# Layer 0's second MLP chunk in seven products for both column halves, with more weight sums in DRAM and wider squares in attention

## The chip, the cores and the metric

One core of one Trainium2 chip runs the whole program. The metric is the device time in microseconds (us) of one execution; a profile of one execution says where it goes. The engines are TensorE (PE, with its weight loads as PEld), VectorE (DVE), ScalarE (ACT), GpSimd (POOL) and SyncE (SP, which here only issues transfers).

## The reference

A trunk of two layers works on x of 256 positions by 2048 channels in float32. Layer 0 mixes by multi-scale pooling and grouped-query attention, layer 1 by a chunkwise mLSTM; behind each mixer stands a gated MLP. Cut to what the change touches:

```python
proj = h @ w_in_ab[e]                          # layer 0: pooling | queries | keys | values
q = apply_rope(rms_norm(q, q_norm[e]), cos, sin)
k = apply_rope(rms_norm(k, k_norm[e]), cos, sin)
...
def conv_ffn(x, w_up, conv_w, conv_b, w_down): # both layers, D_FF = 5632
    u = x @ w_up
    ...                                        # width-3 depthwise convolution over positions
    gate, val = jnp.split(u, 2, axis=-1)
    return (jax.nn.silu(gate) * val) @ w_down
```

## The kernel before, in words

**Precision.** Every float32 product is three matmuls in a reduced format: each operand is split into a high and a low part, and high x high, high x low and low x high are added up in PSUM (the low x low term is left out). Weights come in chunks of 128 x 1024 (512 KB). `Stream` loads them on SP's queue (L114, tile `w`, six chunks ahead), ScalarE casts the high part (L134) and VectorE subtracts for the low part (L135, tile `hl`, two chunks ahead of TensorE, four buffers). All matmuls of products stand on L272.

**The MLP.** The 5632 inner channels are 44 tiles of 128, in K chunks of 4, 8, 8, 8, 8 and 8 tiles (`FCH`). An `up` step makes one tile of gate and value (64 matmuls, four weight chunks) and, on ScalarE and VectorE, the convolution and the gating (L438 to L1019). While the tiles of chunk c + 1 are made, chunk c goes through the down projection. `_ffn_plan` writes the order: up tiles, and in the slots between them the units of the down projection.

**Seven products.** Where a chunk and a column half h (1024 of the 2048 columns) are in `BOTH`, the down projection treats a pair of K tiles, the two blocks of 128 positions and two column blocks of 512 as a 2 x 2 times 2 x 2 product, with seven block products in place of eight. `unit` runs them: an A unit four products for each pair, a B unit three. `combine` makes the combinations of the left operand (L1025 to L1032), `drain` adds the sums in PSUM to accumulators or to x (L1086, L1088), and `total` adds it all up at the end. Where a half is not in `BOTH`, `down` runs the eight products directly (tile `dn`, 48 matmuls for one chunk and one column block) and `residual` (L448) adds them to x. The halves of a chunk that are both in seven products run in units of two pairs; with one half alone they run in units of one pair.

**Sums of weights.** An A unit also needs sums of weight blocks. They come in two ways. On the fly (`Sum` and `Chain`): SP loads one part (L119), an accumulating transfer on POOL's queue adds the other (L120), and VectorE makes the other two sums of a pair in the chunk itself (L130, L131). Or from DRAM: `premix` builds all four sums ahead of time in a scratch tile `m`, in steps that each wait for a matmul (L484): two copies issued by ScalarE, three accumulating steps issued by POOL, each in two halves of the partitions. SP then loads `m` like any weight chunk. A premix starts every 26 units of the planner's clock (about a microsecond each) for the first eight, then every 45, and takes five such gaps of 26. `_ffn_weights` says which pairs are premixed.

**Attention.** `block` takes the projected keys or queries of four heads (tile `kproj` or `qproj`, two position blocks of 512 columns in PSUM), squares them with a sum for each head (eight ScalarE instructions of 128 columns, L519), and applies gains and rotation on VectorE (L528, L529, L531). TensorE transposes the result (L563). It runs for the keys and for three groups of queries.

TensorE runs in the order in which the program is written; the order on the other engines is set by a scheduler.

Of the kernel before, what the change touches and what calls it, by code (L numbers as in the profile page):

```python
# [9 lines left out]
F32 = mybir.dt.float32  # L10
F32R = mybir.dt.float32r
AF = mybir.ActivationFunctionType
ALU = mybir.AluOpType
AX = mybir.AxisListType
PSUM = bass.MemoryType.PSUM

P = 128
# [14 lines left out]
FT = DFF // P  # L32
FCH = [4, 8, 8, 8, 8, 8]
CH = 8
BOTH = ((0, 2, 3, 4), (0, 1, 2, 3, 4))
LAST = (4, 4)

PASSES = (
    ("A1 B1 A0 B0", "A1 B1", "A1 B1 A0 B0", "A1 B1 A0 B0", "A0 A1 A1+ B0 B1 B1+"),
    ("A1 B1 A0 B0", "A1 B1 A0 B0", "A1 B1 A0 B0", "A1 B1 A0 B0", "A0 A1 A1+ B0 B1 B1+"),  # L40
)
NEG = -1.0e30
# [50 lines left out]
class Stream:  # L93
# [60 lines left out]
    def next(self):  # L154
        i = self.at
        self.ahead(i)
        self.at += 1
        return self.hl.pop(i)
# [58 lines left out]
def trunk(ctx: ExitStack, tc: tile.TileContext, gx, xT, xn, call, catt, cml, weights, mixes, out):  # L217
    nc = tc.nc
    v, a, g, pe = nc.vector, nc.scalar, nc.gpsimd, nc.tensor

    def pool(name, bufs, **kw):
        return ctx.enter_context(tc.tile_pool(name=name, bufs=bufs, **kw))
# [9 lines left out]
    sm1 = pool("small1", 1)  # L232
# [41 lines left out]
    def rsqrt(ss, n, scale, name):  # L274

        t = smp.tile([P, n], F32, tag=f"rv{n}", name=f"rv_{name}")
        v.tensor_scalar(t, ss, scale, EPS, ALU.mult, ALU.add)
        y = smp.tile([P, n], F32, tag=f"ry{n}", name=f"ry_{name}")
        g.tensor_tensor(y, t, mhalf[:, :n], ALU.pow)
        e = smp.tile([P, n], F32, tag=f"re{n}", name=f"re_{name}")  # L280
        v.tensor_mul(e, y, y)
        v.tensor_mul(e, e, t)
        v.tensor_scalar(e, e, -0.5, 1.5, ALU.mult, ALU.add)
        v.tensor_mul(e, e, y)
        return e
# [156 lines left out]
    def bc(ap, n):  # L442
        return ap.unsqueeze(1).to_broadcast([ap.shape[0], n, ap.shape[1]])
# [27 lines left out]
    def paced(ins):  # L471

        tc.add_manual_dep(ins.ins, last_mm[0].ins.name, now, reason="paced")

    def premix(layer, gap, late, n):

        def one(i, s0, s1, r, made):
            m = scratch.tile([P, 2, CH * P], F32, tag=f"m{layer}{i}", name=f"m{layer}_{i}")
            h = CH * P // 2
            steps = [(nc.scalar, m[:, 0], s0, {}), (nc.scalar, m[:, 1], r, {}), (g, m[:, 0], s1, add),  # L480
                     (g, m[:, 1, :h], m[:, 0, :h], add), (g, m[:, 1, h:], m[:, 1, :h], add)]
            for n, (eng, to, src, kw) in enumerate(steps):
                for p in range(0, P, P // 2):
                    paced(eng.dma_start(to[p : p + P // 2], src[p : p + P // 2], **kw))  # L484
                    yield (0.1, 0.6, 0.6, 0.6, 0.6)[n] * gap
            for j in range(2):
                made[j].ap = m[:, j]

        for i, e in enumerate(mixes[layer]):
            wv.aside(one(i, *e), min(i + 1, n) * gap + max(i + 1 - n, 0) * late)  # L490
# [8 lines left out]
    def attention_layer(norm, nxt):  # L499
        with ExitStack() as es:  # L500
# [11 lines left out]
            def block(ps, ti, dst, name):  # L512

                rot = tp.tile([P, 2, 512], F32, tag="rot", name=f"rot_{name}")
                ss = smp.tile([P, 8], F32, tag="qss", name=f"qss_{name}")
                sq = sm1.tile([P, 512], F32, tag="sq", name=f"hsq_{name}")[:, :P]
                for t in range(2):
                    for h in range(4):
                        a.activation(sq, ps[:, t, h * P : h * P + P], AF.Square,  # L519
                                     accum_out=ss[:, 4 * t + h : 4 * t + h + 1])  # L520
                for t in range(2):
                    t2 = t1p.tile([P, 512], F32, tag=f"qt2{t}", name=f"qt2_{name}{t}")
                    q4 = ps[:, t, :].rearrange("p (h a b c) -> p h a b c", h=4, a=2, b=2)
                    o4 = t2.rearrange("p (h a b c) -> p h a b c", h=4, a=2, b=2)
                    gs = tab[:, ti + 1, t].rearrange("p (a b c) -> p a b c", a=2, b=2)
                    for b in range(2):
                        gb = gs[:, :, b, :].unsqueeze(1).to_broadcast([P, 4, 2, 32])
                        v.tensor_mul(o4[:, :, :, b, :], q4[:, :, :, 1 - b, :], gb)  # L528
                    v.tensor_mul(rot[:, t, :].rearrange("p (h d) -> p h d", h=4),  # L529
                                 ps[:, t, :].rearrange("p (h d) -> p h d", h=4), bc(tab[:, ti, t], 4))  # L530
                    v.tensor_add(rot[:, t, :], rot[:, t, :], t2)  # L531
                yield 9.5

                def scales():

                    s3 = ss.rearrange("p (t h) -> p t h", t=2)
                    rc = norm.rcol.unsqueeze(2).to_broadcast([P, 2, 4])
                    for _ in range(2):
                        v.tensor_mul(s3, s3, rc)
                    rq = rsqrt(ss, 8, 1.0 / HD, f"q{name}")  # L540
                    r3 = rq.rearrange("p (t h) -> p t h", t=2)
                    v.tensor_mul(r3, r3, rc)
                    return rq

                rq = None
                if name == "k":
                    yield from wv.wait(lambda: norm.blocks == NB)
                    fin = norm.finish()
                    yield next(fin)
                    rq = scales()  # L550
                    yield 4.0
                    for t in range(2):
                        r4 = rot[:, t, :].rearrange("p (h d) -> p h d", h=4)
                        v.tensor_mul(r4, r4, rq[:, 4 * t : 4 * t + 4].unsqueeze(2).to_broadcast([P, 4, P]))
                    yield 3.0
                for h2 in range(2):
                    if name != "k":
                        yield from wv.take("qt")
                    tr = psp.tile([P, 2, S], F32, tag="ps", name=f"tr_{name}{h2}")
                    for h in range(2):  # L560
                        for t in range(2):
                            c = (2 * h2 + h) * P
                            pe.transpose(tr[:, h, t * P : t * P + P], rot[:, t, c : c + P], ident)  # L563
                    d = dst(h2)
                    a.copy(d[:, 0], tr)
                    v.tensor_sub(d[:, 1], tr, d[:, 0].bitcast(F32))
                    if rq is None:
                        rq = scales()
                    yield 0.6
                if name == "k":  # L570
                    yield from fin
                return rq
# [166 lines left out]
            ps = mov_group(xx, "kproj", 512, ahead, tables)  # L739
# [2 lines left out]
            catb.extend(actp.tile([P, 8, 2, S], F32R, tag=f"B{i}", name=f"cat{i}") for i in range(2))  # L742
            wv.add(k_block(ps))
            wv.tick(0.0)
            premix(0, 26.0, 45.0, 8)
            with tc.manual_schedule(engines={mybir.EngineType.SP}):
                ps = mov_group(xx, "qproj0", after=squares)
            wv.add(q_block(ps, 0, 5.5))
            ps = mov_group(xx, "vproj")
# [502 lines left out]
def _halves(layer, c):  # L1252

    return () if c == len(FCH) - 1 else (0, 1) if c in BOTH[layer] else (1,)

# [6 lines left out]
def _direct(layer, c, b):  # L1262

    return LAST[layer] if c == len(FCH) - 1 and b >= NB // 2 else 0
# [67 lines left out]
def _ffn_weights(layer, up, parts):  # L1332

    down = iter(parts[0])
    out, u, mixes = [], 0, []
    for kind, c, i, *j in _ffn_plan(layer):
        if kind == "up":
            out += up[u : u + 4]
            u += 4
        elif kind in ("down", "two"):  # L1340
            n = FCH[c] // 2 - 1
            out += [next(down) for _ in range((n, n + 2)[i] if kind == "two" else (FCH[c] - _direct(layer, c, i)) // 2)]
        elif kind != "mix":
            q0 = sum(FCH[:c]) // 2
            s0, s1, r, ba, bb = parts[1 + 5 * i : 6 + 5 * i]
            js = [q0 + e for e in j[0]]
            if kind == "B":
                last = bb[js[0] // 2]
                out += [ba[q] for q in js] + [last if len(js) == 2 else last[:, js[0] % 2 * 512 : js[0] % 2 * 512 + 512]]
                continue  # L1350
            for q in js:
                if c < len(FCH) - 1 and (q % 2 or i and c == 1 and layer == 0):
                    out += [Sum(s0[q], s1[q]), Chain(r[q])]
                else:
                    made = [Made(), Made()]
                    mixes.append((s0[q], s1[q], r[q], made))
                    out += made
    return out, mixes
# [103 lines left out]
```

## Time and profile before

| | |
|---|---|
| median of 3 runs | 2157.45 us (2157.44 to 2157.64) |
| the profiled execution | 2157.31 us, span 2155.5 us |
| busy | PE 2150.3, DVE 1746.4, ACT 1419.3, POOL 231.1 us |
| TensorE clock granted | 1.00 |
| transfers | 566.78 MB, mean 263 GB/s |
| layer 0: attention, then its MLP | to about 257 us, to about 970 us |
| layer 1: mLSTM, then its MLP | to about 1450 us, to the end |

A row of the groups gives line, engine and operation, output and inputs with their shapes, count, then busy time and mean ns of one, then the idle time before them and what ended it. A row of the stage windows gives the stretch, then busy us and number of instructions of PE, PEld, DVE, ACT and POOL, the granted clock, the mean busy share of the 16 DMA engines and what they moved. The chain of waits is the work that ended last, followed back from the end.

### The profile page before, as it was taken

Reading aid. Unit: us, or ns where it says so; the run is one execution under the profiler, and the core shown is the slowest. Engines: PE = TensorE matmul, PEld = TensorE weight load, DVE = VectorE, ACT = ScalarE, POOL = GpSimd, SP = SyncE. Lnnn points to the kernel's source line nnn. Section 1 sums busy time; section 2 is a strip of 40 time slices with the busy share of each in tenths; the row PEclk is TensorE's granted clock in tenths of the full one; section 3 lists DMA queues with packets and bytes.
Section 4 is the critical chain, followed back from the end, with each engine's and each line's share of the span. In section 5 each row is a group of like instructions: output and inputs, shape, how many; then the busy total and the mean of one; then the engine's idle time right before and its main releaser. Section 6 shows DMA issues by size and latency. Waiting matters only on the chain.

```text
span 2155.5 us, 32062 instructions
## 1 busy us (share of the span) xinstructions
PE 2150.3 (100%) x11412; PEld 1842.8 (85%) x11412; DVE 1746.4 (81%) x2453; ACT 1419.3 (66%) x2223; POOL 231.1 (11%) x294
## 2 busy tenths in 40 slices
PE   9999999999999999999999999999999999999999
PEld 7888888888888888889888888888888888888887
DVE  7686678887988899897777676667888998889988
ACT  7665577766777777766454544457777777776774
POOL 0022111110111100001111111111111000000000
PEclk9999999999999999999999999999999999999999
DMA  9668889898999887778788887888989888877775
GB/s 331 219 203 257 258 243 315 263 300 256 307 300 311 282 275 253 264 267 238 234 256 240 244 248 232 280 245 249 300 276 288 282 264 256 271 251 268 254 250 188
DMA packets 168452, 566.78 MB, mean 263 GB/s; under 512 B 21371, under 2 KB 24227, under 8 KB 168291
## 3 DMA queue, kind: packets, MB, share of 16 engines
q1 hardware_dynamic: 130784, 466.01, 61.6%
q0 software_dynamic: 22624, 56.90, 15.9%
q10 hardware_dynamic: 14882, 41.82, 6.1%
q8 instruction: 89, 1.46, 0.3%
q14 instruction: 73, 0.59, 0.1%
HBM read 562.51 MB, written 77.64 MB: 297 GB/s over the span
## 4 chain that ended last, share of the span: by engine, by line
PE 98%; DVE 1%; issue 0%; ACT 0%; DMA 0%; ACTq 0%; DVEq 0%
PE up L272 45%; PE pp L272 16%; PE op L272 8%; PE mv L272 4%; PE mq L272 4%; PE mk L272 4%; PE mo L272 4%; PE dn L272 4%; PE qproj L272 3%; PE kproj L272 1%; PE vproj L272 1%; PE pool L272 1%; PE av L272 1%; PE qk L272 1%; PE xt L323 0%; DVE hl L135 0%
## 5 line engine op out<-in xcount | busy, mean ns | idle before, releaser
L135 DVE TENSOR_TENSOR hl<-w,hl 128x1024 fp32r<-128x1024 f32 (+1 forms) x847 | 1016.1, 1212 | 212.9 <-ACT hl L134 204.6
L134 ACT CAST hl<-w 128x1024 fp32r<-128x1024 f32 (+1 forms) x846 | 867.3, 1044 | 424.3 <-PE up L272 124.2
L272 PE MATMUL up<-xx,hl 128*128 128x512 f32 (+1 forms) x5632 | 994.1, 337 | 0.1
L272 PEld LDWEIGHTS up<-xx,hl 128*128 128x128 f32 x5632 | 866.8, 188 | 130.8 <-DVE hl L135 0.9
L272 PE MATMUL pp<-hl,s 128*128 128x512 f32 x864 | 214.7, 390 | 0.1
L484 POOL DMA_DIRECT2D m<-m x144 | 116.1, 808 | 688.1 <-PE up L272 287.9
L272 PEld LDWEIGHTS pp<-hl,s 128*128 128x128 f32 x864 | 159.2, 188 | 31.9 <-DVE hl L135 0.9
L272 PE MATMUL pp<-hl,g 128*128 128x512 f32 x648 | 165.1, 390 | 0.0
L272 PEld LDWEIGHTS pp<-hl,g 128*128 128x128 f32 x648 | 119.1, 188 | 23.0
L438 ACT COPY tb_up<-up 128x512 f32<-128x512 f32 x88 | 51.7, 587 | 129.5 <-PE up L272 129.5
L484 POOL DMA_DIRECT2D m<-in_dn x72 | 61.2, 849 | 461.9 <-PE up L272 129.9
L1011 DVE TENSOR_TENSOR y<-y,z 128x510 f32<-128x510 f32 x88 | 60.6, 689 | 58.3 <-ACT y L1010 58.3
L1010 ACT ACTIVATE y<-tb_up,conv 128x256 f32<-128x256 f32 x176 | 103.7, 589 | 0.0
L439 DVE TENSOR_TENSOR tb_up<-up,tb_up 128x512 f32<-128x512 f32 x88 | 60.8, 690 | 44.8 <-ACT tb_up L438 44.6
L272 PE MATMUL mk<-xx,hl 128*128 128x512 f32 (+1 forms) x512 | 92.2, 337 | 0.0
L272 PE MATMUL mq<-xx,hl 128*128 128x512 f32 (+1 forms) x512 | 92.2, 337 | 0.0
L272 PE MATMUL mv<-hl,xx 128*128 128x512 f32 (+2 forms) x480 | 91.8, 350 | 0.0
L272 PE MATMUL op<-hl,cat 128*128 128x512 f32 x384 | 91.5, 393 | 0.0
L272 PE MATMUL mo<-hl,xx 128*128 128x512 f32 x384 | 90.5, 391 | 0.0
L1008 ACT ACTIVATE z<-tb_up,conv 128x256 f32<-128x256 f32 x176 | 88.3, 502 | 2.9 <-DVE tb_up L1003 2.3
L272 PE MATMUL op<-hl,mcat 128*128 128x512 f32 x384 | 89.5, 392 | 0.0
L272 PEld LDWEIGHTS mq<-xx,hl 128*128 128x128 f32 x512 | 79.3, 188 | 11.6
(233 smaller groups left out, 2176.3 us busy)
## 6 DMA issues: line engine op xcount, KB each, us to landing
w<-in_up SPq DMA_DIRECT2D x352, 512.0 KB, 5.3
w<-in_dn SPq DMA_DIRECT2D x174, 512.0 KB, 4.9
w<-in_m_in SPq DMA_DIRECT2D x124, 512.0 KB, 5.1
m<-in_dn ACTq DMA_DIRECT2D x144, 256.0 KB, 5.5
w<-m SPq DMA_DIRECT2D x72, 512.0 KB, 5.1
w<-in_a_in SPq DMA_DIRECT2D x45, 512.0 KB, 5.0
m<-in_dn POOLq DMA_DIRECT2D x72, 256.0 KB, 6.6
m<-m POOLq DMA_DIRECT2D x144, 128.0 KB, 5.6
```

What stands on the lines that cost most here:

```text
L134: (self.nc.vector.tensor_copy if i + c == 0 else self.nc.scalar.copy)(hl[:, 0, c : c + n], w[:, c : c + n])
L135: low = self.nc.vector.tensor_sub(hl[:, 1, c : c + n], w[:, c : c + n], hl[:, 0, c : c + n].bitcast(F32))
L272: last_mm[0] = pe.matmul(out_, lhsT, rhs, start=start, stop=stop, skip_group_check=True)
L438: a.copy(tb, ps[:, :, 1, :])
L439: v.tensor_add(tb, ps[:, :, 0, :], tb)
L484: paced(eng.dma_start(to[p : p + P // 2], src[p : p + P // 2], **kw))
L1008: a.activation(z[:, 0, j, :], u[:, j, :], AF.Copy, scale=cw(tl, 0))
L1010: a.activation(y[:, j, :], u[:, j, :], AF.Identity, scale=cw(tl, 1), bias=cw(tl, 3))
L1011: v.tensor_add(y[:, :, 1:S], y[:, :, 1:S], z[:, 0, :, 0 : S - 1])
```

## The change

1. `BOTH` gains chunk 1 of layer 0 for both halves, and `PASSES` gives it the order `A1 B1 A0 B0`: half 0 of that chunk, direct before, goes in seven products too.
2. All even pairs of chunks before the last get their sums from DRAM. Before, chunk 1 of layer 0 made all four of its half 1 on the fly. Premixes of layer 0 rise from 16 to 20; sums on the fly stay at 4 in that chunk, 36 in all.
3. Premixes after the eighth start every 33 units, not 45.
4. In `block` the squares are one ScalarE instruction for 512 columns, written into `rot`, and VectorE sums each head of them.

```diff
-BOTH = ((0, 2, 3, 4), (0, 1, 2, 3, 4))
+BOTH = ((0, 1, 2, 3, 4), (0, 1, 2, 3, 4))
...
-    ("A1 B1 A0 B0", "A1 B1", "A1 B1 A0 B0", "A1 B1 A0 B0", "A0 A1 A1+ B0 B1 B1+"),
+    ("A1 B1 A0 B0", "A1 B1 A0 B0", "A1 B1 A0 B0", "A1 B1 A0 B0", "A0 A1 A1+ B0 B1 B1+"),
...
-                sq = sm1.tile([P, 512], F32, tag="sq", name=f"hsq_{name}")[:, :P]
                 for t in range(2):
-                    for h in range(4):
-                        a.activation(sq, ps[:, t, h * P : h * P + P], AF.Square,
-                                     accum_out=ss[:, 4 * t + h : 4 * t + h + 1])
+                    a.activation(rot[:, t, :], ps[:, t, :], AF.Square)
...
+                    v.tensor_reduce(ss[:, 4 * t : 4 * t + 4], rot[:, t, :].rearrange("p (h d) -> p h d", h=4),
+                                    AX.X, ALU.add)
                     v.tensor_mul(rot[:, t, :].rearrange("p (h d) -> p h d", h=4),
...
-            premix(0, 26.0, 45.0, 8)
+            premix(0, 26.0, 33.0, 8)
...
-                if c < len(FCH) - 1 and (q % 2 or i and c == 1 and layer == 0):
+                if q % 2 and c < len(FCH) - 1:
                     out += [Sum(s0[q], s1[q]), Chain(r[q])]
```

How it moves the instructions is seen at three places. On TensorE before, behind the second up tile of chunk 2 in layer 0, one pair's A unit of half 1 (`pp`, chunk 1, half 1, products 4, 6, 5, 3) is followed by the direct product of column block 0 (`dn`), twelve matmuls for each weight chunk:

```order
L272 MATMUL pp_1_14_4170<-hl_4242,s_1_1_3562 128x512 x3
L272 MATMUL pp_1_16_4171<-hl_4242,s_1_1_3562 128x512 x3
L272 MATMUL pp_1_15_4172<-hl_4266,s_1_1_3562 128x512 x3
L272 MATMUL pp_1_13_4173<-hl_4266,g_1_2968 128x512 x3
L272 MATMUL dn_1_0_4330<-hl_4306,g_1_2968 128x512 x12
L272 MATMUL dn_1_0_4330<-hl_4321,g_1_2968 128x512 x12
```

On TensorE in the changed kernel, behind the fifth up tile of chunk 2, half 0 of the same chunk runs as an A unit of two pairs, six matmuls for each weight chunk:

```order
L272 MATMUL pp_1_04_4761<-hl_4702,s_1_0_3537 128x512 x3
L272 MATMUL pp_1_06_4762<-hl_4702,s_1_0_3537 128x512 x3
L272 MATMUL pp_1_05_4763<-hl_4723,s_1_0_3537 128x512 x3
L272 MATMUL pp_1_03_4764<-hl_4723,g_1_2948 128x512 x3
L272 MATMUL pp_1_04_4761<-hl_4767,s_1_1_3547 128x512 x3
L272 MATMUL pp_1_06_4762<-hl_4767,s_1_1_3547 128x512 x3
```

The `dn` rows are gone, and the same columns come from `pp` rows that use up a weight chunk in half as many matmuls. On ScalarE before, the squares of the last query group (`hsq_q`) lie scattered between weight casts (`hl`), the softmax (`pr`, `pt`) and a premix copy (`m`):

```order
L519 ACTIVATE hsq_q_1265,qss_q_1264<-qproj_1034 128x128
L134 CAST hl_1324<-w_1171 128x1024
L519 ACTIVATE hsq_q_1265,qss_q_1264<-qproj_1034 128x128 x4
L606 CAST pt_1315<-ptr_1310 128x512
L519 ACTIVATE hsq_q_1265,qss_q_1264<-qproj_1034 128x128
L134 CAST hl_1346<-w_1199 128x1024
L591 ACTIVATE pr_1298,sm_1299<-sc_1288,mx_1295,rs_1197 128x256 x2
L519 ACTIVATE hsq_q_1265,qss_q_1264<-qproj_1034 128x128
L484 DMA m_2_1210<-in_dn 64x1024
L134 CAST hl_1401<-w_1235 128x1024
L519 ACTIVATE hsq_q_1265,qss_q_1264<-qproj_1034 128x128
```

On ScalarE in the changed kernel the same place reads:

```order
L517 ACTIVATE rot_q_1248<-qproj_1024 128x512 x2
L134 CAST hl_1304<-w_1156 128x1024
L685 DMA pw<-in_catt 128x512
L605 CAST pt_1295<-ptr_1290 128x512
L134 CAST hl_1326<-w_1184 128x1024
L484 DMA m_2_1195<-in_dn 64x1024
L590 ACTIVATE pr_1278,sm_1279<-sc_1268,mx_1275,rs_1182 128x256 x2
```

The eight squares became two at the head, with no split between them. On VectorE before, the block's rotation starts behind the split that follows all of these (`hl_1401`):

```order
L135 TENSOR_TENSOR hl_1401<-w_1235,hl_1401 128x1024
L528 TENSOR_TENSOR qt_q_1274<-qproj_1034,tab 128x8x32 x2
L529 TENSOR_TENSOR rot_q_1263<-qproj_1034,tab 128x512
L528 TENSOR_TENSOR qt_q_1279<-qproj_1034,tab 128x8x32 x2
L529 TENSOR_TENSOR rot_q_1263<-qproj_1034,tab 128x512
L539 TENSOR_TENSOR qss_q_1264<-qss_q_1264,re_n_470 128x8
```

On VectorE in the changed kernel it starts with a reduction, ahead of the split `hl_1304`, which is the one called `hl_1324` before:

```order
L526 TENSOR_REDUCE qss_q_1249<-rot_q_1248 128x4
L584 TENSOR_REDUCE mx_1275<-sc_1268 128x2
L525 TENSOR_TENSOR qt_q_1252<-qproj_1024,tab 128x8x32 x2
L526 TENSOR_REDUCE qss_q_1249<-rot_q_1248 128x4
L528 TENSOR_TENSOR rot_q_1248<-qproj_1024,tab 128x512
L525 TENSOR_TENSOR qt_q_1258<-qproj_1024,tab 128x8x32 x2
L586 SCALAR_TENSOR_TENSOR mx_1275<-mx_1275,rs_1182 128x2
L135 TENSOR_TENSOR hl_1304<-w_1156,hl_1304 128x1024
```

The two reductions (L526) are new, and the block's work begins three splits earlier. TensorE's order in attention is the same in both kernels.

## The prediction

> **What bounds the kernel now.** I read the page first, then the waits of TensorE, then the chain of work around the second K chunk of the first gated MLP, then the stage windows and the transfers. On the page:
>
> ```profile
> span 2155.5 us, 32062 instructions
> PE 2150.3 (100%) x11412; PEld 1842.8 (85%) x11412; DVE 1746.4 (81%) x2453; ACT 1419.3 (66%) x2223; POOL 231.1 (11%) x294
> PEclk9999999999999999999999999999999999999999
> ```
>
> TensorE is busy all but 5.2 us of the span, at its full clock throughout. Busy is not the same as fed, so the waits of its weight loads come next (engine, line, what it waited for, then us in total, times, longest):
>
> ```profile
> PEld kproj L272 <- DVE hl L135: 0.9, 3, 0.4
> PEld up L272 <- DVE hl L135: 0.9, 2, 0.5
> PEld pp L272 <- DVE hl L135: 0.9, 2, 0.5
> PEld ptr L604 <- ACT pr L595: 0.7, 2, 0.4
> PEld tr_q L563 <- DVE rot_q L531: 0.4, 1, 0.4
> ```
>
> Behind the first product of the program only 0.9 + 0.9 + 0.7 + 0.4 = 2.9 us are ever waited for. So a matmul taken away is time taken away, as long as the other engines and the transfers keep up; and little can be won in any other way.
>
> **The change, part by part.** *The products.* The chain from 422 us on is unbroken TensorE (start, length, instructions):
>
> ```profile
> 422.17 2.73 PE pp L272 x12
> 424.90 11.14 PE up L272 x64
> 436.04 2.73 PE pp L272 x12
> 438.77 10.88 PE dn L272 x48
> ...
> 499.40 2.05 PE pp L272 x9
> ...
> 552.14 5.45 PE pp L272 x24
> ```
>
> This is chunk 1 of layer 0, from 422.17 to 552.14: 129.97 us. It holds eight up tiles of 11.14, four A units of one pair (2.73), four B units of one pair (2.05) and two direct blocks (10.88). A 512-column matmul thus takes 10.88 / 48 = 0.227 us, and 5.45 / 24 gives the same. The change drops 2 x 48 = 96 dn matmuls and adds 2 x 24 + 2 x 18 = 84 pp ones (A0 and B0). The total of both kinds in the program falls from 360 + 1512 to 264 + 1596: minus 12, or 12 x 0.227 = **2.72 us**. The second layer already runs its chunk 1 in just this form:
>
> ```profile
> 1611.66 5.45 PE pp L272 x24
> ...
> 1738.91 5.45 PE pp L272 x24
> ```
>
> From 1611.66 to 1738.91 are 127.25 us, 2.72 less than 129.97: the same number from a stage that has the new form. I take 2.72 as won.
>
> *VectorE and ScalarE in that chunk.* Splits of weights grow: eight more chunks of 1024 columns, four halves fewer. Drains: four more accumulations and three more additions to x against four residual additions fewer, so three more. Costs (out, in, count, busy, mean ns):
>
> ```profile
> L135 DVE TENSOR_TENSOR hl<-w,hl 128x1024 fp32r<-128x1024 f32 x48 | 57.7, 1219 | 11.2 <-ACT hl L134 11.0
> L135 DVE TENSOR_TENSOR hl<-w,hl 128x512 fp32r<-128x512 f32 x4 | 2.7, 686 | 0.9 <-ACT hl L134 0.9
> L1088 DVE TENSOR_TENSOR acc<-acc,pp 128x512 f32<-128x512 f32 x4 | 2.7, 679 | 0.0
> 422.00:552.00 130.00, 130.00 (x695) 111.62 (x694) 106.88 (x144) 87.54 (x136) 15.15 (x19) 1.00 0.90 279
> 552.00:680.00 128.00, 127.92 (x683) 109.34 (x682) 114.46 (x152) 92.78 (x141) 16.07 (x20) 1.00 0.95 308
> 680.00:807.00 127.00, 127.00 (x681) 109.08 (x680) 114.44 (x151) 92.47 (x140) 12.21 (x15) 1.00 0.89 283
> ```
>
> VectorE: 8 x 1.22 - 4 x 0.69 + 3 x 0.68 = 9.0 us more; its busy time in this stretch is 106.9 of 130 (third pair of the window rows, after PE and PEld), and would be 115.9 at most of 127.25. Chunks 2 and 3 (the next two rows), which have the new form too, show 114.5 of 128 and 114.4 of 127, with TensorE busy 127.92 and 127.00. So this load is hidden beside TensorE at 90% of VectorE; I cost it at 0. If the cover failed, it would be in steps like the largest wait above, 0.5 us each. ScalarE goes from 87.5 to about 92.5 and has more room.
>
> *The squares.* Per block (keys and three query blocks) eight squares of 128 columns with their read of the sum go, and two of 512 come; VectorE gets two reductions. Nearest rows:
>
> ```profile
> L519 ACT ACTIVATE hsq_q<-qproj 128x128 f32<-128x128 f32 x24 | 6.7, 278 | 3.8 <-PE qproj L272 3.4
> L519 ACT ACTIVATION_READ_ACCUMULATOR hsq_q<-qproj 128x1 f32 x24 | 4.8, 199 | 0.0
> L438 ACT COPY tb_pool<-pool 128x512 f32<-128x512 f32 x1 | 0.6, 572 | 0.0
> 140.12 0.68 DVE L531 TENSOR_TENSOR rot_q<-rot_q,qt_q 128x512 f32<-128x512 f32 x1
> ```
>
> ScalarE: 8 x (0.28 + 0.20) = 3.8 us become 2 x 0.57 = 1.1 per block, 2.7 less. The 512-column reduction is not in the trace; no 512-column VectorE operation here is far from 0.68, so 2 x 0.68 = 1.36 us more per block. Bounds on the end: VectorE works without a gap from 134 to 146 us (last query block beside the first pool group), where the waits of tr_q (0.4) and ptr (0.7) lie. If the whole 1.36 falls there, +1.4. If the earlier start of the block's VectorE work (its first reduction now stands three splits ahead of where the block used to begin) removes both waits, -1.1. The two pull against each other; I take 0.
>
> *Sums from DRAM.* Four more premixes. They, and the pace of 33 in place of 45, load the DMA engines. These are the queues in chunk 2 (packets, MB, share of 16 engines), then in the busiest stretch so far, with the weight loads' median landing time:
>
> ```profile
> q1 hardware_dynamic: 8599, 31.33, 65.6%
> q0 software_dynamic: 1941, 5.12, 22.9%
> q10 hardware_dynamic: 880, 2.88, 6.1%
> 325.00:378.00 53.00, 53.00 (x280) 45.37 (x279) 46.06 (x60) 42.23 (x68) 9.63 (x12) 1.00 1.00 316
> q1 hardware_dynamic: 3508, 12.78, 64.5%
> q0 software_dynamic: 1164, 2.89, 29.8%
> q10 hardware_dynamic: 320, 1.05, 5.8%
> w<-in_up SPq DMA_DIRECT2D x16, 512.0 KB, 7.8
> ```
>
> In chunks 1 and 2 the new kernel needs 31.3 MB of weights. q0's 5.12 MB are 4 x 0.52 for sums on the fly and 3.0 of premixes; these and q10's 2.88 grow by 45/33, to 4.1 and 3.9. Together 31.3 + 6.2 + 3.9 = 41.4 MB in 127.25 us, 326 GB/s. Priced by the stretch at share 1.00 (0.645 x 53 / 12.78 = 2.67 us per MB for q1, 5.47 for q0, 2.93 for q10) that is 83.6 + 33.9 + 11.4 = 128.9 us: full, 1.7 us over. Yet at share 1.00 TensorE was busy 53.00 of 53. Weights are fetched six chunks ahead; with 8 x 4 + 28 = 60 chunks in 127.25 us that is some 12.7 us, against a landing time of 7.8. A single ten-microsecond stretch carried more:
>
> ```profile
> 590.00:600.00 10.00, 6.00 (x6) 1.00 1.03 395
> ```
>
> I take 0. Bounds: below, nothing, since before has no transfer that TensorE waits for; above, the dearest rows, in the rivals. The new issues on ScalarE (16) and POOL (24, less than a microsecond each) stand in order before ScalarE's splits and POOL's sums on the fly; the same pattern in chunk 2 left TensorE 0.08 us short.
>
> The Trainium skill's "Perfetto Trace Analysis", section on the roofline, puts a core's share of memory at 358 GB/s and the sixteen engines' ceiling near 435; by that 326 fits and the sum stays. The 395 above agrees that 358 is no wall here.
>
> **Sum.** 2157.31 (the profiled execution, 0.14 under the median of 2157.45) - 2.72 + 0 + 0 + 0 = **2154.6 us**, 0.13% less.
>
> **Rivals.** *Transfers too slow, the slower side.* Place: layer 0 from 422 to 677 us. With the dearest rows seen, q1 as in chunk 3 and q0 as in chunk 1,
>
> ```profile
> q1 hardware_dynamic: 8701, 31.69, 71.9%
> q0 software_dynamic: 1841, 4.83, 22.7%
> ```
>
> 0.719 x 127 / 31.69 = 2.88 and 0.227 x 130 / 4.83 = 6.11 us per MB, the demand is 90.1 + 38.0 + 11.4 = 139.5 us in 127.25: 12.2 late per chunk, two chunks, +24: **2179**. It decides once a load lands later than the 12.7 us of lookahead. Against it: those prices come from stretches that were not full. By the price of the full stretch instead it is 2 x 1.7 = 3.4, so **2158.0**. Here the skill's "DMA: Bandwidth & Descriptors", section "Queues, rings and completion order", speaks against the change: each DMA engine serves the queues that have work in turn, packet by packet, so more premix traffic takes turns from the weights. The rise of the landing time to 7.8 agrees; that TensorE waited, no row of before shows.
>
> *VectorE or ScalarE late.* Gaps like the 0.5 above, one in each of two chunks, and the 1.4 in attention: -2.72 + 2.4, **2157.0**. For it: VectorE at 90%; against: layer 1's five chunks.
>
> *Waits vanish.* All 2.9 us go too: **2151.7**. Against it: three of the four kinds lie where VectorE gets more work.
>
> *The change does not reach the end.* Twelve matmuls go, something else keeps 2157.3. Against it: the chain has TensorE on both sides.
>
> **How the numbers follow.** Forecast 0.58; full-stretch price 0.12; VectorE or ScalarE 0.12; no effect 0.03; waits vanish 0.05; dear transfers 0.10. About 0.2% (4.3 us) is what a measurement of this kernel can tell from no change. Below 2153.1 lies only the fourth case, above 2161.8 only the dear one, so faster 0.05, same 0.85, slower 0.10. The range takes the forecast with the lower bound of attention (2153.5), and the next three cases with 1 us for both causes at once (2159.0), leaving out the two ends, 0.15.
>
> **What would show it.** Right: the pp and dn counts 1596 and 264; chunk 1 taking 127.3 us on the chain; VectorE near 115 there; DMA share about 1.00 from 422 to 677 us with TensorE busy throughout. Wrong: waits of the hl rows on DMA of w, TensorE idle behind VectorE splits in chunks 1 and 2, or a wait of over 1 us in the last query block.

## The result, and the profile after

The changed kernel takes **2154.18 us** (median of 22 runs, 2153.99 to 2154.60) against 2157.49 us (22 runs, 2157.18 to 2157.89) of the kernel before: 3.31 us less, ratio 0.9985 with a 95% interval of 0.9979 to 0.9991. The forecast was 2154.6 us, 2.71 less than the execution profiled before. The page of the changed kernel:

```profile
span 2152.7 us, 32117 instructions
PE 2147.7 (100%) x11400; PEld 1842.3 (86%) x11400; DVE 1760.0 (82%) x2468; ACT 1420.2 (66%) x2171; POOL 250.2 (12%) x318
```

This execution took 2154.60 us, the longest of the 22; what that is about comes below. TensorE has 12 matmuls fewer (11412 to 11400), VectorE 13.6 us more work, GpSimd 24 issues more. The matmuls of the two kinds (line, engine, form, count, busy us, mean ns):

```profile
L272 PE MATMUL pp<-hl,s 128*128 128x512 f32 x912 | 226.5, 390 | 0.2
L272 PE MATMUL pp<-hl,g 128*128 128x512 f32 x684 | 173.9, 390 | 0.0
L272 PE MATMUL dn<-hl,g 128*128 128x512 f32 x264 | 61.1, 390 | 0.0
```

That is 1596 and 264, as forecast. All waits of the weight loads in the whole program, first product included:

```profile
PEld pp L272 <- DVE hl L135: 1.4, 3, 0.6
PEld wps L296 <- DVE pad L700: 1.2, 1, 1.2
PEld ptr L603 <- ACT pr L594: 0.4, 2, 0.3
```

Against before, tr_q and up are gone, ptr has 0.4 in place of 0.7 (at another place, as the point on the squares shows), and pp has grown from 0.9 to 1.4. The waits of kproj lie at the very start and come and go: runs e12 and e14, one kernel twice, have 0.2 and 0.4 of them. The new one of pp is 0.55 us, in the chain at the start of chunk 1 of layer 0:

```profile
421.95 0.50 ACTq L484
...
422.49 0.41 ACT g L1017
422.89 0.49 ACT tb_up L438
...
425.09 1.23 DVE hl L135
...
426.36 1.42 PE pp L272 x5
```

Read backwards: TensorE stops before 426.36 for a split (L135), which had waited for VectorE's work on an up tile (left out here), and that for ScalarE's; ScalarE had first issued a premix copy (L484, 0.50 us) that stands in its order ahead of them. From 550 us on the chain is plain TensorE again. The stage with the most transfers, chunks 1 and 2 (columns as in the windows of before):

```profile
422.00:549.00 127.00, 126.87 (x678) 108.69 (x677) 113.90 (x150) 92.81 (x141) 22.26 (x28) 1.00 0.98 321
549.00:677.00 128.00, 128.00 (x686) 109.99 (x685) 115.55 (x151) 92.74 (x141) 20.33 (x26) 1.00 1.00 322
```

The queues of the first of these windows, and the landing time of the weight loads (least, median, most) in the first and in the second:

```profile
q1 hardware_dynamic: 8473, 30.85, 64.0%
q0 software_dynamic: 2336, 5.90, 25.2%
q10 hardware_dynamic: 1200, 3.93, 8.3%
DMA to landing us min/median/max: 3.5/7.8/11.8
DMA to landing us min/median/max: 3.4/8.3/12.5
```

The transfers run at a share of 0.98 and 1.00, and TensorE is idle 0.13 us, all of it the wait at 426. Where the time went is read by cutting the chain of each profile at the same five events: the first qproj, the start of the long run of up tiles at 267 us (some 10 us into the first MLP), the end of the up tile ahead of chunk 1's first A unit, the first A unit of chunk 2, and the last addition to x.

```profile
28.34 3.85 PE qproj L272 x17
267.01 57.82 PE up L272 x332
549.60 5.45 PE pp L272 x24
2149.29 0.42 DVE x L1135
```

The same rows of the kernel before:

```profile
27.96 4.08 PE qproj L272 x18
267.27 57.82 PE up L272 x332
2152.35 0.42 DVE x L1136
```

| us | before | changed | difference |
|---|---|---|---|
| start, to qproj0 | 27.96 | 28.34 | +0.38 |
| attention and the first up tiles, to 267 | 239.31 | 238.67 | -0.64 |
| chunk 0's time, to 422 | 154.90 | 154.92 | +0.02 |
| chunk 1, to 550 | 129.97 | 127.67 | -2.30 |
| the rest | 1600.21 | 1599.69 | -0.52 |

(Chunk 1 begins at 422.17 before, and at 421.93 now, where the last up tile ends.) The start is no part of the change: a second profile of the same kernel (e13 below) has 28.04, others here 27.7 to 28.38. The table ends with the last addition. From there to the end of the span are 3.2 us before (2155.5 - 2152.35) and 3.4 now (2152.7 - 2149.29); the runs e1 and e13 have 3.4 too, e2 and e5, with their 11412 matmuls, 3.2. What makes this tail longer stays open. Without the start the stages give -3.44, with the tail about -3.2; the medians, -3.31.

### The profile page after: what moved, and what is told of

The parts are those of the page before. It is cut to its first block, busy times and chain, and to the rows that moved or that the text cites. A ratio compares the mean times of both kernels' runs of the same rounds, so it can differ in the third digit from the quotient of the medians.

```text
span 2152.7 us, 32117 instructions
## 1 busy us (share of the span) xinstructions
PE 2147.7 (100%) x11400; PEld 1842.3 (86%) x11400; DVE 1760.0 (82%) x2468; ACT 1420.2 (66%) x2171; POOL 250.2 (12%) x318
## 4 chain that ended last, share of the span: by engine, by line
PE 98%; DVE 1%; issue 0%; ACT 0%; ACTq 0%; DVEq 0%
PE up L272 45%; PE pp L272 16%; PE op L272 8%; PE mv L272 4%; PE mq L272 4%; PE mk L272 4%; PE mo L272 4%; PE qproj L272 3%; PE dn L272 3%; PE kproj L272 1%; PE vproj L272 1%; PE pool L272 1%; PE av L272 1%; PE qk L272 1%; PE xt L323 0%; DVE hl L135 0%
## 5 line engine op out<-in xcount | busy, mean ns | idle before, releaser
L135 DVE TENSOR_TENSOR hl<-w,hl 128x1024 fp32r<-128x1024 f32 (+1 forms) x851 | 1024.0, 1215 | 196.0 <-ACT hl L134 186.1
L272 PE MATMUL pp<-hl,s 128*128 128x512 f32 x912 | 226.5, 390 | 0.2
L484 POOL DMA_DIRECT2D m<-m x160 | 128.3, 820 | 798.2 <-PE up L272 304.0
L272 PEld LDWEIGHTS pp<-hl,s 128*128 128x128 f32 x912 | 168.1, 188 | 34.2 <-DVE hl L135 1.4
L272 PE MATMUL pp<-hl,g 128*128 128x512 f32 x684 | 173.9, 390 | 0.0
L272 PEld LDWEIGHTS pp<-hl,g 128*128 128x128 f32 x684 | 125.9, 188 | 24.3
L438 ACT COPY tb_up<-up 128x512 f32<-128x512 f32 x88 | 51.7, 587 | 123.0 <-PE up L272 123.0
L484 POOL DMA_DIRECT2D m<-in_dn x80 | 71.0, 888 | 357.1 <-PE dn L272 121.2
```

The lines of the kernel that those rows point to most:

```text
L135: low = self.nc.vector.tensor_sub(hl[:, 1, c : c + n], w[:, c : c + n], hl[:, 0, c : c + n].bitcast(F32))
L272: last_mm[0] = pe.matmul(out_, lhsT, rhs, start=start, stop=stop, skip_group_check=True)
L438: a.copy(tb, ps[:, :, 1, :])
```

## The experiments

**Products alone, squares alone.** Run e1 is the changed kernel with the old squares, run e2 the kernel before with the new ones.

```diff
 # e1, on the changed kernel
+                sq = sm1.tile([P, 512], F32, tag="sq", name=f"hsq_{name}")[:, :P]
-                    a.activation(rot[:, t, :], ps[:, t, :], AF.Square)
+                    for h in range(4):
+                        a.activation(sq, ps[:, t, h * P : h * P + P], AF.Square,
+                                     accum_out=ss[:, 4 * t + h : 4 * t + h + 1])
...
-                    v.tensor_reduce(ss[:, 4 * t : 4 * t + 4], rot[:, t, :].rearrange("p (h d) -> p h d", h=4),
-                                    AX.X, ALU.add)
```

(e2 is the same diff the other way round, on the kernel before.)

> The changed kernel with the squares of before (eight ScalarE instructions of 128 columns for each block); products, premixes and pace stay as changed. Theory (the twelve matmuls give 2.72 us, the squares the rest of the 3.31): 2154.5 to 2155.0 us, 2.5 to 3.0 under before, with the waits of tr_q back in attention. Rival (the squares carry the gain and the products are lost to transfers or VectorE): 2156.5 to 2157.5 us. Rival (the squares do nothing at the end and the surplus is the new order of the MLP's waits): 2154.2 us, no difference from the changed kernel.

> The kernel before with the squares of 512 columns alone; its products, its sums on the fly and its pace of 45 stay. Theory: the twelve matmuls are missing, so 2156.8 to 2157.3 us, 0.2 to 0.7 under before, with attention ending about 0.6 us earlier, as in the changed kernel. Rival (the squares carry the gain): 2154.2 to 2155 us. Rival (they do nothing at the end): 2157.5 us.

Measured: e1 2154.94 us, as expected (2157.47 before, beside it: -2.53, ratio 0.9988, 0.9980 to 0.9997), e2 2156.72 us, just under the expected range (-0.75, ratio 0.9996, 0.9987 to 1.0005: by the time alone not told from no change). The two sum to -3.28, against -3.31 for both at once. The stages say it more sharply than the times. In e1:

```profile
28.13 4.08 PE qproj L272 x18
267.44 57.82 PE up L272 x332
422.38 0.50 ACTq L484
550.03 5.45 PE pp L272 x24
```

In e2:

```profile
28.38 3.63 PE qproj L272 x16
267.01 57.82 PE up L272 x332
421.91 2.73 PE pp L272 x12
551.89 5.45 PE pp L272 x24
```

Attention takes 239.31 in e1, as before, and 238.63 in e2, as changed: the 0.64 to 0.68 us come from the squares. Chunk 1 (from 422.36, where e1's last up tile ends, and from 421.91) takes 127.67 and 129.98: the 2.30 come from the change in the MLP (products, sums and pace together, which e1 has and e2 lacks), and so does the rest, 1599.59 in e1 and 1600.21 in e2. In e2 the two waits of up of the kernel before (0.9) are there, in e1 they are not. They lie in chunk 2: from its first A unit to the unit behind its fifth up tile are 80.81 us before (552.14 to 632.95) and 80.21 now (549.60 to 629.81). They stood behind splits, and the order around these is another now; which move took them away was not traced.

**The same step back in layer 1.** Run e5 makes half 0 of chunk 1 in layer 1 direct again.

```diff
-BOTH = ((0, 1, 2, 3, 4), (0, 1, 2, 3, 4))
+BOTH = ((0, 1, 2, 3, 4), (0, 2, 3, 4))
...
-    ("A1 B1 A0 B0", "A1 B1 A0 B0", "A1 B1 A0 B0", "A1 B1 A0 B0", "A0 A1 A1+ B0 B1 B1+"),
+    ("A1 B1 A0 B0", "A1 B1", "A1 B1 A0 B0", "A1 B1 A0 B0", "A0 A1 A1+ B0 B1 B1+"),
```

(the second line of `PASSES`)

> The changed kernel with half 0 of chunk 1 in layer 1 direct again, the same step back in another place: 12 matmuls more, and less VectorE work and fewer sums there. Theory (a matmul more is 0.227 us more, wherever it stands): 2.72 us over the changed kernel, 2156.6 to 2157.2. Rival (what a matmul is worth depends on what else the stage waits for): anything under 2 us or over 3.5 us more.

Measured: 2156.40 us, 2.22 over the changed kernel, under the expected range. In the profile that chunk lasts from 1608.06 to 1738.03, 129.97 us, against 127.26 (1608.58 to 1735.84) in the changed kernel: 2.71 where the twelve matmuls stand. The missing 0.5 us can be placed with e13, the second profile of the changed kernel, which at 2154.22 us lies near the median: against it e5 starts 0.18 us earlier (27.86 against 28.04), and its tail behind the last addition is about 0.25 shorter (3.2 against 3.4), which leaves under 0.1. So a stage gives a matmul's price to a hundredth, and a whole time only to some half microsecond.

**What the sums from DRAM are for.** Run e3 keeps the seven products but makes all of chunk 1's sums on the fly, eight in place of four.

```diff
-                if q % 2 and c < len(FCH) - 1:
+                if c < len(FCH) - 1 and (q % 2 or c == 1 and layer == 0):
...
-            premix(0, 26.0, 33.0, 8)
+            premix(0, 26.0, 45.0, 8)
```

> The changed kernel with the sums of all four pairs of chunk 1 in layer 0 made on the fly for both halves (8 in place of 4), 16 premixes in place of 20, and the pace of 45. VectorE gets 4 x 1.36 = 5.4 us more in chunk 1, about 119 of 127 us, and the accumulating transfers and copies get fewer bytes. Theory (VectorE is hidden up to there, and transfers cost nothing at either rate): 2154.0 to 2154.8 us, as the changed kernel within 0.5. Rival (VectorE is at the edge in chunk 1): gaps of some 0.5 us behind hl in chunk 1, 2155 to 2156.5 us. Rival (the transfers of the 20 premixes at the pace of 33 cost something now): 2153 us or less.

Measured: **2163.55 us**, 9.4 over the changed kernel and slower than before (ratio 1.0031, 1.0019 to 1.0042). None of the three expectations came near. The chain of e3 at the second A unit of chunk 1:

```profile
419.81 1.23 DVE hl L135
...
421.07 10.21 DMA sum<-in_dn
...
431.86 7.24 DMA sum<-in_dn
...
439.12 0.69 DVE w L130
...
441.00 1.29 PE pp L272 x4
```

A sum on the fly is two transfers one behind the other, a plain one (10.21 us) and an accumulating one (7.24). The first starts at 421, just when a split of an earlier sum ends and frees its buffer; the tile sum has two. Where a unit covers two pairs and both sums are on the fly, both buffers are used up in each unit, and the next unit is 16.6 us away. All three stops of TensorE in chunk 1 (0.5, 1.9 and 2.8 us) lead back to a sum in this way. The row of VectorE ahead of the longest one, with its idle time in brackets:

```profile
502.07 0.69 DVE L130 TENSOR_TENSOR w<-w,sum 128x512 f32<-128x512 f32 x1 [6.16 <-DMA sum<-in_dn]
```

At 431 and 439 us the same line had idled 1.67 and 3.44 us. So VectorE was not late from too much work; it waited. That gave a new theory, with two runs and a control. Run e7 is e3 with three buffers, e9 the control with the same smaller store of raw weights, e8 the changed kernel with one buffer.

```diff
 # e7, on e3 (e9: the last two edits on the changed kernel; e8: bufs=1 there)
-        w = self.sums.tile([P, CH * P], F32, tag="sum", bufs=2, name=f"sum{i}")
+        w = self.sums.tile([P, CH * P], F32, tag="sum", bufs=3, name=f"sum{i}")
...
-    wp = pool("wraw", 7)
+    wp = pool("wraw", 6)
...
-    st = Stream(nc, behind, wp, sp, weights, 6, 2)
+    st = Stream(nc, behind, wp, sp, weights, 5, 2)
```

> The kernel of run e3 (eight sums on the fly in chunk 1, 2163.6 us) with three buffers for the tile sum in place of two, and the room for it taken from the raw weights (six buffers and five chunks ahead, not seven and six). In run e3 the chain showed 10.2 + 7.2 us of the plain and the accumulating transfer of sum one behind the other, starting when a buffer came free at 421 us. Theory (two sums in each A unit use up both buffers, so that the next unit's sums start too late): with a third buffer most of the loss goes, 2154 to 2158 us, or within 2 us of the control run e9. Rival (VectorE's 5.4 us more in chunk 1 are the loss): still 2161 to 2165 us. Rival (the accumulating transfers are too slow at a full share): still 2161 to 2165 us.

> The changed kernel with one buffer for sum in place of two; VectorE's work, the transfers and the order stay. Two A units of a half are 16.6 us apart, and one sum takes 6.3 + 8.8 = 15.1 us to land (medians around chunk 1 in the changed kernel) behind the moment its buffer is free, plus about 3 us of sums and splits on VectorE. Theory (buffers and the sum's latency set what run e3 lost): 1 to 4 us lost at the second A unit of most halves of the chunks with sums on the fly, some 18 places, so 2165 to 2220 us. Rival (VectorE or transfers were the loss, buffers don't matter): 2154 to 2155 us.

> The changed kernel with raw weights loaded five chunks ahead in six buffers, not six in seven: the control for run e7, and a test of the transfers' slack. Five chunks of 127.25 / 60 = 2.12 us are 10.6 us on average against a landing time of 8.0 to 8.5 us in chunks 1 and 2. Theory (transfers near a full share land in time with room to spare): 2154.0 to 2155.5 us. Rival (the slack is nearly used up, transfers are the next bound): waits of TensorE behind DMA of w from 422 to 677 us, 2157 us or more.

Measured: e7 2159.06 us (over 2158, but within 2 us of its control), the control e9 2159.29 us, e8 2217.92 us, in its range. At the same VectorE work as e3, and with one weight chunk less ahead, the third buffer wins back 4.5 of the 9.4 us. The 4.9 that are left are as much as the control loses, but that they are the same loss is not shown: e9 has the changed kernel's 20 premixes at the pace of 33, e7 has e3's 16 at 45, and the chain of e7 in chunk 1 still passes through a sum:

```profile
491.60 8.67 DMA sum<-in_dn
```

VectorE idled 4.25 us until it had landed, and TensorE stopped for 0.94, 0.87 and 0.61 us behind it. So three buffers shorten the stops and do not end them. With one buffer, and the VectorE work and transfers of the changed kernel, 63.7 us are lost, nearly all at A units (TensorE's waits in e8, then two pieces of its chain in chunk 1):

```profile
PEld pp L272 <- DVE hl L135: 67.9, 64, 4.1
```

```profile
488.46 6.11 DMA sum<-in_dn
...
495.14 10.90 DMA sum<-in_dn
```

The row of the waits names VectorE's split, and VectorE is not the cause: in chunks 1 and 2 it sat idle 23.3 us, four times, until a sum had landed. So the buffers and the 15 to 17.5 us of a sum's two transfers set what e3 and e8 lose, and getting the even pairs' sums from DRAM is what lets units of two pairs run without a stop.

**How near the edge the transfers are.** The control e9 missed its own expectation (2154.0 to 2155.5): with five chunks ahead, 10.6 us, it is 5.1 us slower than the changed kernel. In its chunk 1 ScalarE's casts waited 7.2 us for weight chunks to land; in the changed kernel they never did there. Run e10 packs the same premixes more densely; run e11 puts all of chunk 1's sums into DRAM.

```diff
 # e10
-            premix(0, 26.0, 33.0, 8)
+            premix(0, 26.0, 20.0, 8)
 # e11
-            premix(0, 26.0, 33.0, 8)
+            premix(0, 26.0, 24.0, 8)
...
-                if q % 2 and c < len(FCH) - 1:
+                if q % 2 and c < len(FCH) - 1 and not (c == 1 and layer == 0):
```

> The changed kernel with a premix every 20 units in place of 33 once the first eight are through; the same 20 premixes, only closer together. By chunk 1's rows (q1 30.85 MB at 64.0% of 127 us, q0 5.90 MB at 25.2%, q10 3.93 MB at 8.3%) and the premixes' part of q0 and all of q10 times 1.65 the demand becomes about 81 + 32 x 1.4 + 10.5 x 1.65 = 143 us in 127. Theory as on record (the price of the full stretch holds, and a demand over the share makes loads late): waits behind DMA of w, 5 to 25 us more, 2159 to 2180. Rival (premixes give way to weights, or the price falls with the load): 2154 to 2155 us. That also tells how far the pace of 33 is from the edge.

> The changed kernel with no sums on the fly in chunk 1 of layer 0: all its sums from DRAM, 24 premixes in layer 0 in place of 20, one every 24 units after the eighth so that they come in time. VectorE loses 4 x 1.36 = 5.4 us in chunk 1; the premixes' transfers run 33/24 = 1.4 times as densely. Theory (transfers are at their edge in chunk 1, as runs e9 and e10 showed; VectorE and the buffers are not): loads of w land later than the 12.7 us of lookahead in places, 2157 to 2166 us. Rival (VectorE is what limits chunk 1, and the transfers still have room): 2153.5 to 2154.2 us.

Measured: e10 **2167.57 us** (+13.4, in its range), e11 2155.00 us (+0.8, between its two expectations). Chunk 1 in e10, and the landing of its weight loads:

```profile
422.00:549.00 127.00, 120.86 (x624) 99.79 (x623) 103.48 (x137) 85.32 (x129) 30.29 (x38) 1.00 1.03 327
DMA to landing us min/median/max: 6.3/11.4/16.2
```

Chunk 2 in e11, its densest:

```profile
549.00:677.00 128.00, 127.81 (x680) 108.60 (x679) 113.00 (x149) 93.35 (x140) 27.27 (x34) 1.00 1.04 340
DMA to landing us min/median/max: 6.2/9.5/14.1
```

Chunk 1 in e9:

```profile
422.00:549.00 127.00, 124.33 (x657) 105.31 (x656) 108.33 (x143) 91.47 (x139) 20.99 (x26) 1.00 0.97 310
DMA to landing us min/median/max: 3.4/8.4/12.9
```

The DMA share hardly tells these apart (0.98, 1.03, 1.04, 0.97); the longest landing beside the lookahead puts them in order. In the changed kernel it is 11.8 in chunk 1 and 12.5 in chunk 2 against 12.7 us, and TensorE waits for no weight load. In e11 14.1: 0.2 us idle. In e9 12.9 against 10.6: 2.7 (in the profiled execution, which at 2166.3 us was the longest of its ten; they scatter from 2157.4). In e10 16.2, with a median of 11.4: 6.1. Not all that e10 loses is late weights, though. At 375 and at 441 us ScalarE had idled 4.19 and 3.64 us behind a premix copy (L484) that waited for its matmul, with a finished up tile to be read (L438); stops of TensorE of 1.3 us, ahead of chunk 1, and of 0.9 us follow. And the order is a rough gauge. The lookahead is an average over a chunk, and e11's longest load passed it at almost no cost. Denser premixes don't always lengthen the landing either: in e12 below, denser than the changed kernel and at a share of 1.02, the longest are 10.3 and 9.5 us in chunks 1 and 2. So the changed kernel lies near an edge that e9 and e10 cross, and how much slack it has is not known to a microsecond. The Trainium skill's "DMA: Bandwidth & Descriptors", section "Queues, rings and completion order", has each DMA engine take turns between the queues that have work; the trace agrees, since in e10 the weights did not get ahead of the denser premixes: their median landing rose from 7.8 to 11.4 us. The turns themselves no view here shows.

**The new wait.** Run e12 only moves the paced copies: 30 units in place of 33. e13 and e14 are the changed kernel and e12 again, beside each other.

```diff
-            premix(0, 26.0, 33.0, 8)
+            premix(0, 26.0, 30.0, 8)
```

> The changed kernel with the pace of 30 in place of 33 after the eighth premix. The copy issued by ScalarE that stands on the chain at 421.95 us (0.50 us, ahead of a wait of 0.55 at the first A unit of chunk 1) is due earlier, and the premixes' transfers are 1.1 times as dense, with the longest landing of a weight chunk in chunk 1 now 11.8 us against 12.7 of lookahead. Theory (that wait depends on where the paced issue falls, and there is about 1 us of slack in the transfers): 2153.6 to 2155.5 us, a loss of up to 1 us if landings pass 12.7, a gain of 0.4 if only the wait goes. Rival (33 is already past the edge): over 2156 us.

> The changed kernel unaltered, beside run e14 on the same chip, so that the two can be told apart. Theory (its median repeats): 2154.0 to 2154.4 us, and in its profile the wait of some 0.5 us at the first A unit of chunk 1 in layer 0 is there again, with qproj0 starting anywhere from 27.8 to 28.4 us. Rival (the start at 28.34 us belongs to this kernel and not to one execution): it starts at 28.3 to 28.4 again.

> The kernel of run e12 (pace of 30) again, beside the changed kernel. Theory (moving the paced copies frees the wait of 0.42 to 0.55 us at the start of chunk 1 and costs nothing elsewhere): 0.3 to 0.6 us under run e13, 2153.5 to 2154.0. Rival (run e12's 2153.66 was scatter): within 0.2 us of run e13.

Measured: e12 2153.66 us, e14 **2153.59 us** (11 runs, 2153.43 to 2154.03), e13 2154.22 us (11 runs, 2153.97 to 2156.54), all three in the ranges of their theories: 0.63 us less beside each other, a little over the 0.3 to 0.6 expected. Chunk 1 in e12 begins without a stop:

```profile
419.99 1.51 PE up L272 x9
421.50 5.45 PE pp L272 x24
```

It lasts 127.27 us there (421.50 to 548.77), as the prediction had it, and the wait of pp in the list of waits is 0.9 again. ScalarE reads the finished up tile (L438) 0.04 us behind its end there (421.54), and 0.87 us behind it in the changed kernel (422.80). In e13 the wait is there as in the first profile, and the start is at 28.04, so 28.34 belonged to one execution. The pace of 30 is the fastest kernel of this study.

## Why the prediction was right, point by point

- *Twelve matmuls at 0.227 us, 2.72 won.* Right, shown by 2.71 in the stage of e5 and by chunk 1 of e12, 127.27 against 129.97 before.
- *Chunk 1 takes 127.3 us.* 127.67: the 0.42 more is a wait that the prediction had not named, a premix copy issued by ScalarE ahead of the work that the first A unit needs. The prediction counted these issues ("stand in order before ScalarE's splits") and took them as harmless from chunk 2. What it missed was not their number but where one of them falls. e12 shows it: move them, and chunk 1 takes 127.27. The prediction's list of signs of being wrong has TensorE idle behind VectorE's splits in chunks 1 and 2; that sign came, at 0.13 us idle, and ScalarE's order was behind it.
- *VectorE and ScalarE hidden.* Right but for those 0.42 us: 113.9 of 127 us (forecast at most 115.9), ScalarE 92.8 (forecast 92.5). How much more VectorE would bear no run shows: e3 and e7 add 5.4 us to it, but together with sums on the fly.
- *The squares, 0 between +1.4 and -1.1.* The size was off: -0.64 in the stage, -0.75 in e2's time. Both prices were near (line, form, count, busy us, mean ns):

```profile
L526 DVE TENSOR_REDUCE qss_q<-rot_q 128x4 f32<-128x512 f32 x6 | 4.1, 681 | 2.9 <-ACT rot_q L517 2.9
L517 ACT ACTIVATE rot_q<-qproj 128x512 f32<-128x512 f32 x6 | 3.3, 596 | 3.6 <-PE qproj L272 3.3 <-issue 0.2
```

  The reduction takes 0.68 as assumed, the wide square 0.60 against 0.57. The two effects did pull against each other, as the prediction has it; what it had wrong is that they cancel. Both waits of before in the last query block went, tr_q (0.4) and ptr (0.7, at 145 us), which is the whole lower bound of 1.1. A new wait of ptr (0.18 and 0.25) came at 137 us, where the block's work, now earlier, stands on VectorE ahead of a step that the softmax needs (L530 at 135.63 us, L592 at 136.24). Before, then changed:

```profile
145.15 0.14 PEld L604 LDWEIGHTS ptr<-cst,pr 128*128 128x128 f32 x1 [0.44 <-ACT pr L595]
136.99 0.14 PEld L603 LDWEIGHTS ptr<-cst,pr 128*128 128x128 f32 x1 [0.18 <-ACT pr L594]
```

  In the waits that is 1.1 less and 0.43 more, close to the 0.64 of the stage.
- *Transfers, 0.* Right: no weight load was waited for, though the longest landing of chunk 2 (12.5 us) came near the lookahead. The sum there said 128.9 us of demand in 127.25, and it came out at 0.98 of 127: 40.7 MB moved and not 41.4, and each queue's price was a little lower (2.63, 5.42 and 2.68 us per MB). The rival of dear transfers was no fancy: e10 is in part that case, at +13 us.
- *Waits vanish* was priced as a rival in whole; 0.52 us of it came true in chunk 2, where the waits of up went. That was luck of the order, not worked out.
- *What the prediction left out:* it costed the even pairs' sums from DRAM as a load on the transfers only. It never asked what units of two pairs would do without them; e3 gives the answer, 9.4 us.

So 2154.6 was near partly by cancelling: -0.64 and -0.52 that were not forecast, +0.42 that was not either. That the profiled execution took 2154.60 to the hundredth is luck: its start (+0.38) and its tail (+0.24) make up the difference.

## What to carry to other kernels

When TensorE is busy all the time, a matmul removed is worth its pitch, whether the helpers get busier or not, until a buffer or a landing time runs out; so ask of each helper how long it takes from a free buffer to usable data, and set that beside the distance to the next use. The longest landing against the lookahead is a rough sign of how near the transfers are to the edge; the DMA share of 1.00 is none. A small issue placed in front of urgent work on an engine with time to spare can still stop TensorE, and moving it cost nothing here.

## What was not expected of the hardware

In e3 two stops of TensorE cost more than their length. The stretch around the first (PE, PEld, DVE, ACT, POOL, granted clock, DMA share, GB/s):

```profile
438.00:441.00 3.00, 1.07 (x7) 0.66 (x6) 1.88 (x3) 1.53 (x2) 0.00 (x0) 1.00 1.05 312
441.00:443.00 2.00, 2.00 (x7) 1.59 (x8) 2.00 (x4) 0.00 (x0) 0.00 (x0) 0.74 0.81 200
443.00:446.00 3.00, 3.00 (x10) 2.41 (x9) 3.00 (x5) 2.64 (x3) 0.86 (x1) 0.60 0.96 311
```

After 1.93 us without a matmul the granted clock was 0.74 and then 0.60 (means of the stretches), and the chain has 23 matmuls of the A unit in 7.13 us (from 441.00), where the changed kernel runs 24 in 5.45: about 1.9 us lost on top of the stop. Over chunk 1 e3's TensorE was idle 5.2 us, against 0.1 in the changed kernel, which leaves some 3 of its 8.4 us of longer span (2161.1 against 2152.7) to the slower clock. In e9 and e10, whose waits are 1.6 us at most, it stayed at 1.00 in these windows. The length of a stop alone does not decide: in e8 the clock fell after stops of 3.83 us (to a mean of 0.58 from 509 to 513 us) and 2.32 us (0.73 from 577 to 579), and stayed at 1.00 after stops of 2.15 us at 709 and 777 us. The Trainium skill's "TensorE: Matmul & The Clock Gate", Part 1, names an idle window of about 3.4 us for the fall to half clock; this trace shows a fall after a shorter stop, and the measurement decides. What exactly sets it off was not tried.
